# Squares and sub-norm factors moved to ScalarE, adaptive weights requested together, other tiles for the last expert

## The chip, the cores and the metric

The kernel runs on one core of a Trainium2 chip. A core has five engines that each work through their own list of instructions in order: TensorE (PE, matrix products; PEld in the profile is its weight load), VectorE (DVE), ScalarE (ACT), GpSimd (POOL) and SyncE (SP, which here issues nearly all DMA transfers). The metric is the device time of one execution in microseconds; less is better.

## The reference, cut to what matters

Two transformer blocks on 1024 tokens of width 1024, in fp32. The first has adaptive norms, a convolved two-way mLSTM with a Fourier branch, and 16 experts that each choose 128 tokens. The second has an even layer (differential attention A, forgetting attention B) and an odd layer (sliding window C, banded D). What the change touches:

```python
mx = (silu(c) @ w_ada + b_ada)[:, None, :]          # mc the same from c_ctx
sh1, sc1, ga1, sh2, sc2, ga2 = split(mx, 6)
pc = modulate(rmsnorm(ctx, g_norm1), csh1, csc1) @ w_in
px = modulate(rmsnorm(x, g_norm1), sh1, sc1) @ w_in
...
y = einsum('becf,efd->becd', hid, w_down) * vals    # experts: gather, SwiGLU, scatter-add
return zeros_like(h).at[bidx, idx].add(y)
...
aq, ak = rms_norm(aq, a_qn_g), rms_norm(ak, a_kn_g)  # per head of 64; the same for B, C, D
w = p[:, :, 0] - lam * p[:, :, 1]                    # A: difference of two softmaxes
o = rms_norm(einsum("bhqk,bkhe->bqhe", w, v), a_subln_g) * (1.0 - lam_init)
a_out = o * silu(ag)
```

## The kernel before, in words

A matrix product in fp32 is made of three products (`mm3`, L198 to L200): both operands are split into a high and a low part, the high part by a copy on ACT (L205) and the low part by a subtraction on DVE (L210). So each weight tile costs ACT about as long as DVE, and TensorE works three times. The framework puts each engine's instructions in one fixed order. An instruction waits for what it reads, and for its buffer: a tile name has a small number of buffers, and the next use of one waits for the last reader.

**The start** (`start`). Tokens (`x`, four tiles of 128x1024 first) are scaled by their norm, transposed by TensorE, and kept as `xr`. The adaptive vectors come from eight blocks of `w_ada` (128x8x256, 1 MB each, `wt`): five are multiplied on TensorE (L395, 16 narrow instructions a block), blocks 0, 2 and 5 on DVE (L387, L389, 16 each). From their sum come shift `sh` and scale `A` (L421 to L423). `modulated` (L344 to L347) then makes `y`, its high part `hh` and its low part `hl`; the first weight chunk's product (`pV`) starts when the first `hh` is there. `wt` has four buffers, so blocks 4 to 7 are loaded as blocks 0 to 3 are used up.

**The experts.** Expert e's gate, up and down products go through PSUM tiles `pge`, `pue`, `pde` (one buffer each). DVE scales a down product into `ye` (one buffer), and POOL scatter-adds it to memory in two halves (`xacc`, L1150). The last expert goes through `last_down` (L1153 on): both column halves c0 and c1 are computed apart, each one scaled by DVE (L1164) and scattered at once. Block 2 reads the sum back (`nx`).

**Block 2** is a planned stream of slots: attention items and, between them, the weight products of the next unit. Units A run from about 1470 to 1820 us, B to 2030, an output product, then key/value products, C, and D to the end. A unit's query/key chunk is evicted by ACT as `zq` (L1497); POOL squares it into `hsq` (L1504, one buffer); DVE sums the squares per head (L1505). The same buffer holds `osq` (L2001), ACT's squares of an attention result in A. In A the gates (`vg`) are multiplied by the sub-norm weights on POOL (L1724), and after four row blocks by the sub-norm's reciprocal roots `ory` (L1708, POOL, 128x512). `mixed` transposes the gated result and ACT evicts it as `so` (L1576). POOL also clears `ql` (L1542).

Of the kernel before, what the change touches and what calls it, by code (L numbers as in the profile page):

```python
# [47 lines left out]
def host_arrays(i):  # L48
    f = np.float32
# [42 lines left out]
    for q in range(4):  # L92
# [23 lines left out]
        "gln_o": g["odd_ln_g_2"][0],  # L116
        "subln": g["a_subln_g_2"][0],
        "gcols": np.concatenate([col(g["g_final"]), col(g["even_ln_g_2"][0])], axis=1),
# [39 lines left out]
class Kern:  # L158
# [154 lines left out]
    def start(self, P, hp, cp, xr):  # L313
# [10 lines left out]
        def load_x(t):  # L324
            xs[t] = P.tile([128, D], F32, name="x", bufs=6)
            src = a["x"][t * 128:(t + 1) * 128, :] if t < NT else a["ctx"][(t - NT) * 128:(t - NT + 1) * 128, :]
            nc.sync.dma_start(out=xs[t], in_=src)

        def load_w(b):
            wts[b] = P.tile([128, 8, 256], F32, name="wt", bufs=4)  # L330
            nc.sync.dma_start(out=wts[b], in_=a["w_ada"][b])

        self.hl, self.cl = Slabs([[None] * 2 for k in range(8)], 512), Slabs([[None] for k in range(8)], CTX)

        def modulated(k, g, x):

            c, hi, lo, pool, n = (0, self.hh, self.hl, hp, 512) if g < 2 else (1, self.ch, self.cl, cp, CTX)
            y = P.tile([128, 512], F32, name="y", bufs=3)[:, :n]
            h = hi[:, k, g % 2 * n:(g % 2 + 1) * n]
            if g:  # L340
                nc.scalar.activation(y, x, AF.Identity, bias=sh[:, k, c:c + 1], scale=A[:, k, c:c + 1])
                (nc.gpsimd.tensor_copy(h, y) if k % 3 == 2 else nc.scalar.activation(h, y, AF.Copy))
            else:
                nc.vector.tensor_scalar(y, x, A[:, k, c:c + 1], sh[:, k, c:c + 1], op0=OP.mult, op1=OP.add)  # L344
                nc.scalar.activation(h, y, AF.Copy)
            l = lo.tiles[k][g % 2] = pool.tile([128, n], F32R, name=f"hl{k}{g}" if c == 0 else f"cl{k}")
            (nc.gpsimd if k % 3 == 2 and g == 0 else nc.vector).tensor_tensor(l, y, h.bitcast(F32), op=OP.subtract)  # L347

# [27 lines left out]
        def ada(b):  # L376
            w = wts.pop(b)
            pc = self.ps.tile([128, 2, 2], F32, name="pc", tag="nu", bufs=3)
            if b in ON_DVE or b in ON_POOL:
                eng = nc.vector if b in ON_DVE else nc.gpsimd  # L380
                both = P.tile([128, 512], F32, name="ac", tag="y", bufs=3)
                for c in range(2):
                    ac = both[:, c * 256:(c + 1) * 256]
                    for k in range(8):
                        f = cs[:, k, c:c + 1]
                        if k == 0:
                            eng.tensor_scalar(ac, w[:, k], f, None, op0=OP.mult)  # L387
                        else:
                            eng.scalar_tensor_tensor(ac, w[:, k], f, ac, op0=OP.mult, op1=OP.add)  # L389
                    for i in range(2):  # L390
                        nc.tensor.matmul(pc[:, i, c:c + 1], ac[:, i * 128:(i + 1) * 128], one, start=True, stop=True)
            else:
                pa = self.ps.tile([128, 512], F32, name="pa", tag="mm", bufs=3)
                for k in range(8):
                    nc.tensor.matmul(pa[:2, :256], cs[:, k], w[:, k], start=k == 0, stop=k == 7)  # L395
                row = P.tile([2, 256], F32, name="arow", bufs=2)
                nc.vector.tensor_copy(row, pa[:2, :256])
                for i in range(2):
                    nc.tensor.transpose(pc[:, i], row[:, i * 128:(i + 1) * 128], self.ident[:2, :2])
            nc.vector.tensor_copy(ad[:, 2 * b:2 * b + 2], pc)  # L400

        for t in range(4):
            load_x(t)
        for b in range(4):
            load_w(b)
        tokens(0)
        for b in range(8):
            ada(b)
            if b + 4 < 8:
                load_w(b + 4)  # L410
            if b in (2, 3):
                self.stream[0].dma(b - 2)
        for t in range(4, 10):
            load_x(t)
        for j in range(2):
            self.stream[0].split(j, "pool")
        sh = P.tile([128, 8, 2], F32, name="sh")
# [642 lines left out]
    def experts(self, s):  # L1060
# [92 lines left out]
        def last_down(e):  # L1153
            pd = self.ps.tile([128, D], F32, name="pde", tag="pde", bufs=1)
            y = xp.tile([128, D], F32, name="ye", bufs=1)
            xh, xl = hs.pop(e)
# [198 lines left out]
    def even_consts(self, s):  # L1355
# [6 lines left out]
        pl = self.ps.tile([128, 512], F32, name="pl", tag="tr")  # L1362
        self.sub = ep.tile([128, 128], F32, name="sub")
        ones = ep.tile([64, 128], F32, name="lamo")
# [9 lines left out]

        def later():
            nc.gpsimd.dma_start(out=self.sub, in_=a["subln"].unsqueeze(0).to_broadcast([128, 128]))
            nc.gpsimd.tensor_scalar(self.sub, self.sub, 1.0 - lam_init, None, op0=OP.mult)
            nc.gpsimd.dma_start(out=self.cm, in_=a["cmask"])

        self.event(1, later)  # L1380
        self.ga = ep.tile([128, 4], F32, name="ga")
# [84 lines left out]
class Unit:  # L1466
# [33 lines left out]
    def squares(self, t, n):  # L1500
        K, nc, i = self.K, self.K.nc, t % 4
        sq = K.ap_.tile([128, 256], F32, name="hsq", tag="hsq", bufs=1)
        z = self.zq[t // 4][:, i, :n * 64]
        nc.gpsimd.tensor_tensor(sq[:, :n * 64], z, z, op=OP.mult)  # L1504
        nc.vector.tensor_reduce(self.ss[t // 4][:, i, :n], sq[:, :n * 64].rearrange("p (n d) -> p n d", d=64), op=OP.add, axis=mybir.AxisListType.X)  # L1505
# [57 lines left out]
    def mixed(self, g):  # L1563
# [10 lines left out]
        for i in range(2):  # L1574
            so = K.ap_.tile([128, 256], F32, name="so", tag="oxt", bufs=2)
            nc.scalar.activation(so, pt[:, i * 256:(i + 1) * 256], AF.Copy, scale=0.5)  # L1576
            nc.sync.dma_start(out=self.mx[self.u][:, g * 512 + i * 256:g * 512 + (i + 1) * 256], in_=so)
# [109 lines left out]
class UnitA(Unit):  # L1687
# [11 lines left out]
    def done(self, b):  # L1699
# [6 lines left out]
        r = K.rsqrt(K.up, ss, [128, 4], "or")  # L1706
        gt = self.gt[:, g * 4:g * 4 + 4]
        nc.gpsimd.tensor_tensor(gt, gt, r.unsqueeze(2).to_broadcast([128, 4, 128]), op=OP.mult)  # L1708
        K.event(K.slot_no + 2, lambda: self.mixed(g))

    def heads_in(self, ps, t, n):
        super().heads_in(ps, t, n)
        if self.h == 0:
# [311 lines left out]
```

## Time and profile before

| | us |
|---|---|
| three runs | 2799.67, 2801.87 (median), 2805.9 |
| the profiled execution, its own time | 2794.87 |
| its span in the trace | 2792.8 |
| outside the span | 2.07 |
| TensorE busy | 2649.0 (95%) |
| VectorE busy | 2006.8 (72%) |
| ScalarE busy | 1346.2 (48%) |
| GpSimd busy | 303.8 (11%) |

The granted clock of TensorE over the span is 0.984 of full speed. The busy share is an average over stages. The profile's line numbers are those of the kernel before; the changed code has the same statements a few lines further down.

### The profile page before, as it was taken

How to read it: one execution, taken by the hardware profiler on the slowest of the kernel's cores; microseconds unless marked ns; L12 is line 12 of the kernel's file. 1: busy time of each engine (PE TensorE's matmuls, PEld its weight loads, DVE VectorE, ACT ScalarE, POOL GpSimd, SP SyncE). 2: the span in 40 equal slices, each digit the busy share in tenths (PEclk: the TensorE clock that was granted, in tenths of full speed). 3: DMA queues.
4: the chain of work that ended last, by engine and by line, in shares of the span. 5: the costliest groups of instructions: out<-in, count | busy, mean ns of one | idle time of the engine just before them, and what ended most of it. 6: DMA issues, size and time to landing. Idle time of an engine off the chain costs nothing.

```text
span 2792.8 us, 48578 instructions
## 1 busy us (share of the span) xinstructions
PE 2649.0 (95%) x18222; PEld 2412.0 (86%) x18222; DVE 2006.8 (72%) x4981; ACT 1346.2 (48%) x2589; POOL 303.8 (11%) x413
## 2 busy tenths in 40 slices
PE   6999999999975999999979999999999999999999
PEld 3998897788974888888868999999989999999999
DVE  6676775558468999999968777766674777766652
ACT  4422332223233888877756545444453356544440
POOL 1000000000011111111122212111110000100000
PEclk9999999999987999999989999999999999999999
DMA  6222856655648999999942111211134322221143
GB/s 242 70 87 88 250 176 213 217 195 181 213 156 321 362 395 394 395 395 386 361 124 77 46 47 54 62 58 54 54 98 147 107 80 68 75 63 59 52 115 100
DMA packets 229708, 463.41 MB, mean 166 GB/s; under 512 B 19217, under 2 KB 121777, under 8 KB 228450
## 3 DMA queue, kind: packets, MB, share of 16 engines
q1 hardware_dynamic: 213218, 427.68, 43.9%
q0 software_dynamic: 7296, 17.96, 2.7%
q10 hardware_dynamic: 8960, 14.69, 2.3%
q8 instruction: 143, 2.34, 0.4%
q14 instruction: 91, 0.75, 0.1%
HBM read 387.80 MB, written 55.67 MB: 159 GB/s over the span
## 4 chain that ended last, share of the span: by engine, by line
PE 76%; DVE 10%; DMA 4%; issue 4%; ACT 4%; POOL 1%; SPq 1%; ACTq 0%; DVEq 0%; POOLq 0%
PE pz L198 7%; PE pz L200 7%; PE pz L199 7%; PE po L1954 5%; PE pT L199 3%; PE pT L198 3%; PE pT L200 3%; PE ptp L1940 2%; PE pge L198 2%; PE pge L200 2%; PE pge L199 2%; PE pue L199 2%; PE pue L200 2%; PE pue L198 2%; PE pde L199 2%
## 5 line engine op out<-in xcount | busy, mean ns | idle before, releaser
L198 PE MATMUL pz<-lwh,lh 128*128 128x256 f32 (+1 forms) x2368 | 678.6, 287 | 6.6 <-ACT lh L205 5.0
L200 PE MATMUL pz<-lwh,ll 128*128 128x256 f32 (+1 forms) x2368 | 668.2, 282 | 3.1 <-DVE ll L210 2.0
L199 PE MATMUL pz<-lwl,lh 128*128 128x256 f32 (+1 forms) x2368 | 670.7, 283 | 0.0
L198 PEld LDWEIGHTS pz<-lwh,lh 128*128 128x128 f32 x2368 | 448.2, 189 | 11.2 <-ACT lh L205 6.4
L200 PEld LDWEIGHTS pz<-lwh,ll 128*128 128x128 f32 x2368 | 448.0, 189 | 5.1 <-DVE ll L210 3.5
L199 PEld LDWEIGHTS pz<-lwl,lh 128*128 128x128 f32 x2368 | 449.1, 190 | 1.9
L210 DVE TENSOR_TENSOR ewl<-ewr,ewh 128x1024 fp32r<-128x1024 f32 x372 | 435.3, 1219 | 11.0 <-ACT ewh L205 4.7
L205 ACT ACTIVATE ewh<-ewr 128x1024 fp32r<-128x1024 f32 x378 | 390.6, 1061 | 74.7 <-PE pue L200 23.4
L1923 ACT ACTIVATE S<-S,mx 128x128 f32<-128x128 f32 (+2 forms) x192 | 125.8, 655 | 176.1 <-DVE mx L1898 144.7
L205 ACT ACTIVATE lwh<-lwr 128x1024 fp32r<-128x1024 f32 x130 | 135.8, 1054 | 99.8 <-PE pT L199 47.6
L210 DVE TENSOR_TENSOR lwl<-lwr,lwh 128x1024 fp32r<-128x1024 f32 x128 | 155.7, 1222 | 33.8 <-ACT lwh L205 33.1
L1954 PE MATMUL po<-vg,PT 128*128 128x64 f32 (+1 forms) x1344 | 173.6, 271 | 1.7 <-DVE PT L1945 1.2
L1887 DVE CUSTOM_DVE_ANT_0 S<-psc,bias 128x512 f32<-128x512 f32 (+3 forms) x336 | 161.4, 495 | 14.3 <-PE psc L1885 13.3
L1954 PEld LDWEIGHTS po<-vg,PT 128*128 128x128 f32 x1344 | 165.4, 192 | 5.2 <-ACT PT L1947 2.4
L198 PE MATMUL pT<-hh,lwh 128*128 128x512 f32 x384 | 155.8, 406 | 0.0
L199 PE MATMUL pT<-hl,lwh 128*128 128x512 f32 x384 | 153.3, 399 | 0.0
L200 PE MATMUL pT<-hh,lwl 128*128 128x512 f32 x384 | 152.6, 397 | 0.0
L1504 POOL TENSOR_TENSOR hsq<-zq 128x256 f32<-128x256 f32 (+1 forms) x136 | 84.7, 623 | 560.4 <-ACT zq L1497 267.2
L1884 PE MATMUL psc<-kY,qh 128*128 128x512 f32 (+3 forms) x352 | 128.4, 369 | 12.5 <-DVE mx L1887 9.9
L1940 PE MATMUL ptp<-pack,S 128*128 128x128 f32 x792 | 132.3, 276 | 7.4 <-ACT so L1576 4.6
L1150 POOL DMA_INDIRECT xacc<-ye,idx x32 | 70.5, 2203 | 437.4 <-DVE ye L1145 426.0
L1961 DVE SCALAR_TENSOR_TENSOR vg<-po,l,vg 128x64 f32<-128x64 f32 x192 | 54.0, 281 | 83.4 <-PE po L1954 81.8
(577 smaller groups left out, 6165.6 us busy)
## 6 DMA issues: line engine op xcount, KB each, us to landing
ewr<-in_w_gate_e SPq DMA_DIRECT2D x63, 1024.0 KB
ewr<-in_w_up_e SPq DMA_DIRECT2D x63, 1024.0 KB
ewr<-in_w_down_e SPq DMA_DIRECT2D x63, 1024.0 KB
lwr<-in_w_in SPq DMA_DIRECT2D x36, 512.0 KB
awt<-in_w_ada SPq DMA_DIRECT2D x32, 512.0 KB
lwr<-in_even_w_in SPq DMA_DIRECT2D x32, 512.0 KB
lwr<-in_odd_w_in SPq DMA_DIRECT2D x26, 512.0 KB
wt<-in_w_ada SPq DMA_DIRECT2D x8, 1024.0 KB
```

The costliest lines, as they stand in the source:

```text
L198: nc.tensor.matmul(out, ah, bh, start=start, stop=False)
L199: nc.tensor.matmul(out, ah, bl, start=False, stop=False)
L200: nc.tensor.matmul(out, al, bh, start=False, stop=stop)
L205: nc.scalar.activation(hi, raw, AF.Copy)
L210: (nc.vector if lo_eng == "dve" else nc.gpsimd).tensor_tensor(lo, raw, hi.bitcast(F32), op=OP.subtract)
L1150: nc.gpsimd.indirect_dma_start(out=self.xacc[c][:, :], out_offset=bass.IndirectOffsetOnAxis(ap=idx[:, e:e + 1], axis=0), in_=y[:, c * 512: ...
L1504: nc.gpsimd.tensor_tensor(sq[:, :n * 64], z, z, op=OP.mult)
L1884: nc.tensor.matmul(ps[:, :n], qh, k[:, ks], start=True, stop=False)
L1887: nc.vector.tensor_tensor_reduce(S[:, lo:hi], ps[:, lo - c0:hi - c0], bias, scale, -3e38, OP.add, OP.max, accum_out=mx[:, n_mx:n_mx + 1])
L1923: nc.scalar.activation(S[:, :nk], S[:, :nk], AF.Exp, bias=m, accum_out=l[:, 0:1])
L1940: nc.tensor.transpose(pt[:, i * 128:(i + 1) * 128], S[:, c0 + i * 128:c0 + (i + 1) * 128], K.ident)
L1954: nc.tensor.matmul(po[:, :dv], self.PT[i // 4][:, (i % 4) * 128:(i % 4 + 1) * 128], v(self.k0 // 128 + i), start=i == 0, stop=i == m - 1)
```

## The change

In `start` all eight blocks of `w_ada` are requested at once, ahead of the first chunk's weights and the other tokens. Blocks 0 to 4 get five `wt` buffers; 5 and 6 arrive in four pieces and 7 in eight, in tiles that later hold `hl` and `cl`. `x` has four buffers in place of six. POOL does nothing there any more: the two weight subtractions (L210) and the `hl` subtractions go to DVE, the casts to ACT, and the odd `y` of the second token group stay on ACT while the even ones go to DVE.

In `last_down` the product uses `pge` and the scaled rows use a buffer of the gathered rows `xe`.

In block 2 `squares` uses ACT. The sub-norm weights, now one column, are the scale of the `so` eviction; the multiplication of the gates by them is gone. The factor `ory` is applied by four ACT copies of 128x128. The mask `cm` is loaded by SP.

```diff
         def load_w(b):
-            wts[b] = P.tile([128, 8, 256], F32, name="wt", bufs=4)
-            nc.sync.dma_start(out=wts[b], in_=a["w_ada"][b])
+            if b < 5:
+                w = P.tile([128, 8, 256], F32, name="wt", bufs=5)
+                nc.sync.dma_start(out=w, in_=a["w_ada"][b])
+                wts[b] = [w[:, k] for k in range(8)]
+                return
+            wts[b] = []
+            for i in range(4 if b < 7 else 8):
+                n = 2 if b < 7 else 1
+                w = hp.tile([128, n, 256], F32, name=f"wt{b}{i}", tag=f"hl{(b - 5) * 4 + i}1") if b < 7 else cp.tile([128, n, 256], F32, name=f"wt{b}{i}", tag=f"cl{i}")
+                nc.sync.dma_start(out=w, in_=a["w_ada"][b][:, n * i:n * i + n])
+                wts[b] += [w[:, k] for k in range(n)]
...
-            if g:
+            if g == 2 or g and k % 2:
                 nc.scalar.activation(y, x, AF.Identity, bias=sh[:, k, c:c + 1], scale=A[:, k, c:c + 1])
-                (nc.gpsimd.tensor_copy(h, y) if k % 3 == 2 else nc.scalar.activation(h, y, AF.Copy))
             else:
                 nc.vector.tensor_scalar(y, x, A[:, k, c:c + 1], sh[:, k, c:c + 1], op0=OP.mult, op1=OP.add)
-                nc.scalar.activation(h, y, AF.Copy)
+            nc.scalar.activation(h, y, AF.Copy)
...
-            (nc.gpsimd if k % 3 == 2 and g == 0 else nc.vector).tensor_tensor(l, y, h.bitcast(F32), op=OP.subtract)
+            nc.vector.tensor_tensor(l, y, h.bitcast(F32), op=OP.subtract)
...
-        for b in range(4):
+        for b in range(8):
             load_w(b)
+        for j in range(2):
+            self.stream[0].dma(j)
         tokens(0)
         for b in range(8):
             ada(b)
-            if b + 4 < 8:
-                load_w(b + 4)
-            if b in (2, 3):
-                self.stream[0].dma(b - 2)
         for t in range(4, 10):
             load_x(t)
         for j in range(2):
-            self.stream[0].split(j, "pool")
+            self.stream[0].split(j)
...
         def last_down(e):
-            pd = self.ps.tile([128, D], F32, name="pde", tag="pde", bufs=1)
-            y = xp.tile([128, D], F32, name="ye", bufs=1)
+            pd = self.ps.tile([128, D], F32, name="pde", tag="pge", bufs=1)
+            y = xp.tile([128, D], F32, name="ye", tag="xe")
...
         z = self.zq[t // 4][:, i, :n * 64]
-        nc.gpsimd.tensor_tensor(sq[:, :n * 64], z, z, op=OP.mult)
+        nc.scalar.activation(sq[:, :n * 64], z, AF.Square)
...
-            nc.scalar.activation(so, pt[:, i * 256:(i + 1) * 256], AF.Copy, scale=0.5)
+            nc.scalar.activation(so, pt[:, i * 256:(i + 1) * 256], AF.Copy, scale=K.sub if self.kind == "a" else 0.5)
...
-        gt = self.gt[:, g * 4:g * 4 + 4]
-        nc.gpsimd.tensor_tensor(gt, gt, r.unsqueeze(2).to_broadcast([128, 4, 128]), op=OP.mult)
+        for i in range(4):
+            gt = self.gt[:, g * 4 + i]
+            nc.scalar.activation(gt, gt, AF.Copy, scale=r[:, i:i + 1])
...
-    def gate_in(self, t):
-        super().gate_in(t)
-        K = self.K
-        K.nc.gpsimd.tensor_tensor(self.gt[:, t], self.gt[:, t], K.sub, op=OP.mult)
```

Three places where the order of instructions differs. The first is VectorE at the end of the adaptive vectors (`arow` and `ad` are a block's row and its transposed columns, `lwl` the low part of the first chunk's weights). Before:

```order
L389 SCALAR_TENSOR_TENSOR ac<-wt,cs,ac 128x256 x9
L397 COPY arow<-pa 2x256
L400 COPY ad<-pc 128x4 x2
L397 COPY arow<-pa 2x256
L400 COPY ad<-pc 128x4
L422 TENSOR_TENSOR A<-ad,pack_100 128x16
L423 SCALAR_TENSOR_TENSOR A<-A,pack_100 128x16
L344 TENSOR_SCALAR y<-xr_89,A,sh 128x512
```

Now:

```order
L406 COPY arow<-pa 2x256
L409 COPY ad<-pc 128x4 x2
L406 COPY arow<-pa 2x256
L210 TENSOR_TENSOR lwl<-lwr,lwh 128x8x128
L409 COPY ad<-pc 128x4
L429 TENSOR_TENSOR A<-ad,pack_100 128x16
L430 SCALAR_TENSOR_TENSOR A<-A,pack_100 128x16
L210 TENSOR_TENSOR lwl<-lwr,lwh 128x8x128
L353 TENSOR_SCALAR y<-xr_89,A,sh 128x512
```

The two weight subtractions, which POOL had, now stand between the last block's row and the first `y`.

The second place is ScalarE in a unit A, around the end of a row group (`S` are the exponentials of a row block, `PT` the transposed weights on their way out of PSUM). Before:

```order
L1984 ACTIVATE S,l<-S,mx 128x896 x2
L1497 ACTIVATE zq<-pz 128x256 x2
L1576 ACTIVATE so<-ptm 128x256 x2
L1497 ACTIVATE zq<-pz 128x256
L2001 ACTIVATE osq,oss<-po,l 128x128
L1947 ACTIVATE PT<-ptp 128x256
L1984 ACTIVATE S,l<-S,mx 128x1024 x2
```

Now:

```order
L1983 ACTIVATE S,l<-S,mx 128x896 x2
L1712 ACTIVATE vg<-vg,ory 128x128 x4
L1500 ACTIVATE zq<-pz 128x256
L1507 ACTIVATE hsq<-zq 128x256
L1500 ACTIVATE zq<-pz 128x256
L1507 ACTIVATE hsq<-zq 128x256
L1579 ACTIVATE so<-ptm,sub 128x256 x2
L1500 ACTIVATE zq<-pz 128x256
L1507 ACTIVATE hsq<-zq 128x256
L2000 ACTIVATE osq,oss<-po,l 128x128
L1946 ACTIVATE PT<-ptp 128x256
L1983 ACTIVATE S,l<-S,mx 128x1024 x2
```

A square follows each `zq`, and the four factor copies stand ahead of the `so` evictions.

The third is VectorE at the same `osq` (`mx` is a row maximum, `ISA` the instruction that adds the bias and takes it). Before:

```order
L1520 TENSOR_TENSOR hry<-hry,rt 128x16
L1523 TENSOR_TENSOR zq<-zq,hry 128x256 x4
L1505 TENSOR_REDUCE hss<-hsq 128x4
L2003 SCALAR_TENSOR_TENSOR vg<-po,l,vg 128x128
L1945 COPY PT<-ptp 128x512
L1887 ISA S,mx<-psc,bias 128x512
```

Now:

```order
L1523 TENSOR_TENSOR hry<-hry,rt 128x16
L1526 TENSOR_TENSOR zq<-zq,hry 128x256 x4
L1508 TENSOR_REDUCE hss<-hsq 128x4
L1944 COPY PT<-ptp 128x512
L2002 SCALAR_TENSOR_TENSOR vg<-po,l,vg 128x128
L1886 ISA S,mx<-psc,bias 128x512
```

The copy of `PT`, which does not depend on `osq`, now stands ahead of the multiplication that does.

## Rows read from the trace of the kernel before

**Rows 1.** The page: engine busy times, and VectorE's weight subtractions in the first stages.

```profile
PE 2649.0 (95%) x18222; PEld 2412.0 (86%) x18222; DVE 2006.8 (72%) x4981; ACT 1346.2 (48%) x2589; POOL 303.8 (11%) x413
...
L210 DVE TENSOR_TENSOR lwl<-lwr,lwh 128x1024 fp32r<-128x1024 f32 x128 | 155.7, 1222 | 33.8 <-ACT lwh L205 33.1
```

**Rows 2.** Windows of the core: busy by engine (instructions), TensorE clock, DMA share, GB/s.

```profile
20.00:30.00 10.00, 10.00 (x57) 5.25 (x56) 7.18 (x21) 3.94 (x8) 0.00 (x0) 1.00 0.42 129
...
40.00:50.00 10.00, 7.48 (x31) 3.11 (x30) 4.18 (x10) 3.36 (x5) 3.26 (x2) 0.83 1.01 409
...
1400.00:1470.00 70.00, 56.12 (x252) 45.57 (x251) 43.49 (x60) 36.95 (x55) 16.62 (x12) 0.83 0.43 123
1610.00:1680.00 70.00, 66.65 (x535) 64.36 (x533) 53.98 (x187) 34.90 (x87) 14.29 (x22) 1.00 0.16 45
1890.00:1960.00 70.00, 70.00 (x590) 69.02 (x589) 44.59 (x168) 31.40 (x67) 12.97 (x23) 1.00 0.20 62
```

**Rows 3.** Timeline of TensorE, start: start, duration, line, names, [idle before <-released by].

```profile
33.97 2.75 PE L395 MATMUL pa<-wt,cs 128*2 128x256 f32 x12
...
42.71 0.58 PE L391 MATMUL pc<-one,ac 128*128 128x1 f32 x4 [2.52 <-DVE ac L389]
...
44.96 5.30 PE L395 MATMUL pa<-wt,cs 128*2 128x256 f32 x16
...
53.03 0.39 PE L198 MATMUL pV<-lwh,hh 128*128 128x272 f32 x1 [1.99 <-ACT hh L345]
...
55.62 0.39 PE L200 MATMUL pV<-lwh,hl 128*128 128x272 f32 x1 [0.47 <-POOL hl L347]
```

**Rows 4.** Timeline of VectorE, start.

```profile
37.62 5.86 DVE L389 SCALAR_TENSOR_TENSOR ac<-wt,cs,ac 128x256 f32<-128x256 f32 x9
...
51.77 1.46 DVE L344 TENSOR_SCALAR y<-xr,A,sh 128x512 f32<-128x512 f32 x3
```

**Rows 5.** Timeline of TensorE, last expert.

```profile
1419.84 0.47 PE L198 MATMUL pde<-ewh,xth 128*128 128x512 f32 x1 [1.86 <-DVE ye L1145]
...
1432.02 0.76 PE L198 MATMUL pde<-ewh,xth 128*128 128x512 f32 x1 [4.87 <-DVE ye L1164]
```

**Rows 6.** Timeline of VectorE, last expert.

```profile
1431.12 0.75 DVE L1164 SCALAR_TENSOR_TENSOR ye<-pde,val,ga 128x512 f32<-128x512 f32 x1 [6.90 <-DMA xacc<-ye,idx]
...
1440.54 0.75 DVE L1164 SCALAR_TENSOR_TENSOR ye<-pde,val,ga 128x512 f32<-128x512 f32 x1 [5.87 <-PE pde L200]
```

**Rows 7.** Timeline of GpSimd, last expert.

```profile
1441.58 1.70 POOL L1150 DMA_INDIRECT xacc<-ye,idx  x1 [2.15 <-DVE nlam L1372]
```

**Rows 8.** Waits of TensorE, units A: total us, times, longest.

```profile
PE psc L1884 <- DVE mx L1887: 9.9, 9, 1.7
...
PE ptp L1940 <- ACT so L1576: 3.3, 3, 1.2
```

**Rows 9.** Timeline of TensorE, around one osq of a unit A.

```profile
1629.53 0.50 PE L1884 MATMUL psc<-kY,qh 128*128 128x512 f32 x1 [1.73 <-DVE mx L1887]
```

**Rows 10.** Timeline of ScalarE, the same place in a unit A.

```profile
1627.42 0.37 ACT L2001 ACTIVATE osq<-po,l 128x128 f32<-128x128 f32 x1 [2.61 <-DVE hss L1505]
```

**Rows 11.** Timeline of VectorE, two places in a unit A.

```profile
1605.15 0.42 DVE L1505 TENSOR_REDUCE hss<-hsq 128x4 f32<-128x256 f32 x1 [0.92 <-POOL hsq L1504]
...
1624.75 0.18 DVE L193 SCALAR_TENSOR_TENSOR hry<-hrt,hry 128x16 f32<-128x16 f32 x1
1624.96 0.58 DVE L1520 TENSOR_TENSOR hry<-hry,rt 128x16 f32<-128x16 f32 x1
```

**Rows 12.** Instructions of ScalarE's squares in the output product.

```profile
L1645 ACT ACTIVATE hsq<-oxt x12: 407/418/419, 2085.6 to 2171.2; 128x256 f32<-128x256 f32 x12
```

**Rows 13.** Instructions of the squares' line: ns min/median/max.

```profile
L1504 POOL TENSOR_TENSOR hsq<-zq x136: 398/612/1628, 1468.0 to 2636.2; 128x256 f32<-128x256 f32 x104, 128x128 f32<-128x128 f32 x32
```

**Rows 14.** Timeline of GpSimd, end of a row group, unit A.

```profile
1577.92 1.04 POOL L1708 TENSOR_TENSOR vg<-vg,ory 128x512 f32<-128x512 f32 x1 [5.36 <-DVE ory L193]
```

**Rows 15.** Table loads of ScalarE at the gates' line.

```profile
L1510 ACT ACT_TABLE_LOAD  x1: 1283/1283/1283, 1504.1 to 1504.1; - x1
```

More of the change, by code (lines that the diff above doesn't have):

```diff
@@ L33, in _pack @@
     PACK_W[which] += n
-for _n, _w in (("ident", 128), ("bbf", 8), ("qkg", 8), ("lam", 4), ("sinks", 8), ("cc", 16)):
+for _n, _w in (("ident", 128), ("bbf", 8), ("qkg", 8), ("lam", 4), ("sinks", 8), ("cc", 16), ("subln", 1)):
     _pack(_n, _w, 0)
@@ L80, in host_arrays @@
     put("ident", np.eye(128, dtype=f))
+    put("subln", g["a_subln_g_2"][0][:, None])
     s, j = np.meshgrid(np.arange(128), np.arange(128), indexing="ij")
@@ L116, in host_arrays @@
         "gln_o": g["odd_ln_g_2"][0],
-        "subln": g["a_subln_g_2"][0],
         "gcols": np.concatenate([col(g["g_final"]), col(g["even_ln_g_2"][0])], axis=1),
@@ L324, in load_x @@
         def load_x(t):
-            xs[t] = P.tile([128, D], F32, name="x", bufs=6)
+            xs[t] = P.tile([128, D], F32, name="x", bufs=4)
             src = a["x"][t * 128:(t + 1) * 128, :] if t < NT else a["ctx"][(t - NT) * 128:(t - NT + 1) * 128, :]
@@ L386, in ada @@
                         if k == 0:
-                            eng.tensor_scalar(ac, w[:, k], f, None, op0=OP.mult)
+                            eng.tensor_scalar(ac, w[k], f, None, op0=OP.mult)
                         else:
-                            eng.scalar_tensor_tensor(ac, w[:, k], f, ac, op0=OP.mult, op1=OP.add)
+                            eng.scalar_tensor_tensor(ac, w[k], f, ac, op0=OP.mult, op1=OP.add)
                     for i in range(2):
@@ L394, in ada @@
                 for k in range(8):
-                    nc.tensor.matmul(pa[:2, :256], cs[:, k], w[:, k], start=k == 0, stop=k == 7)
+                    nc.tensor.matmul(pa[:2, :256], cs[:, k], w[k], start=k == 0, stop=k == 7)
                 row = P.tile([2, 256], F32, name="arow", bufs=2)
@@ L1362, in even_consts @@
         pl = self.ps.tile([128, 512], F32, name="pl", tag="tr")
-        self.sub = ep.tile([128, 128], F32, name="sub")
+        self.sub = ep.tile([128, 1], F32, name="sub")
         ones = ep.tile([64, 128], F32, name="lamo")
@@ L1373, in even_consts @@
         self.cm = ep.tile([128, 128], F32, name="cm")
[L1375 to L1380, printed above, removed]
+        self.event(1, lambda: nc.sync.dma_start(out=self.cm, in_=a["cmask"]))
+        nc.vector.tensor_scalar(self.sub, self.col("subln"), 0.5 * (1.0 - lam_init), None, op0=OP.mult)
         self.ga = ep.tile([128, 4], F32, name="ga")
```

## The prediction, made before the changed kernel ran

> **What bounds the kernel now.** I began with the page: TensorE is busy for 95% of the span, every other engine for 72% or less [rows 1]. So an edit pays only where TensorE stands idle or runs at the lower of its two clocks (1.2 against 2.4 GHz). The windows say where that is [rows 2]: at the start, 7.48 of 10 us busy at a granted clock of 0.83 between 40 and 50; where the experts end, 56.12 of 70 us, again at 0.83; a little in units A, 66.65 of 70. Units B are full, 70.00 of 70. Then I read in the timelines and waits of those three places what ended each wait.
>
> **The start.** Between 40 and 50 us TensorE first waits 2.52 us for block 5's products on VectorE, and then multiplies block 7 for 5.30 us, where twelve such instructions took 2.75 before it, 0.229 each, so that sixteen are worth 3.67 [rows 3]. The engine had just been idle when the clock fell. The link is not the limit: it is full between 40 and 50, yet 0.42 busy between 20 and 30, where TensorE works without a pause [rows 2]. With all blocks requested at once their data come early enough for block 5 (nine of its VectorE steps, which took 5.86 us [rows 4], can run sooner and without GpSimd beside them) and blocks 6 and 7 follow each other. I take off the wait and the slow stretch: 2.52 + 1.63 = 4.15 us.
>
> Against it VectorE takes over GpSimd's two weight subtractions, 1.22 us each [rows 1], and the order puts both between block 7's row and the first `y`, which stood at 51.77 [rows 4]. Behind it waits TensorE's first `pV` (53.03, 1.99 us idle [rows 3]). Of the 2.44 us about 0.5 fill a pause in which VectorE waits for block 7's columns; 1.94 are added. GpSimd's `hl` subtractions go: two waits like that of 0.47 at 55.62 [rows 3], -0.94. The `ctx` tokens now load only when `x`'s four buffers come free, and their scaling comes late: no row shows it, it costs between nothing and 1.46 us (three 128x512 passes of VectorE [rows 4]); I take 0.65, near the middle, since transposes of other tokens cover part. On SP the eight blocks now stand ahead of the first weights, which lie ready long before `pV` either way. Sum: -4.15 + 1.94 - 0.94 + 0.65 = -2.5 us. Bounds: +1.6 if the slow clock merely moves to the first product (+1.63) and `ctx` costs its 1.46; -6 if the subtractions hide entirely.
>
> **The last expert.** Its first half waits 1.86 us, because `pde` is still read by VectorE's scaling of the expert before; the second half waits 4.87 us [rows 5], because VectorE could not write `ye` (it waited 6.90 us for the scatter that still reads it) and so did not release the first half's sums [rows 6]. With `pge` and an `xe` buffer neither applies: -6.73 us. The first half took 7.31 us (1419.84 to 1432.02 less 4.87), the second 8.52 (to 1440.54); without the pause in front of it the second should be no slower than the first, -1.2. Together -7.9. What is late next is the scatter: the second half's started at 1441.58 [rows 7]. A scatter into the same half of `xacc` follows the former expert's, which had landed by 1431.12 [rows 6]; two more of some 1.7 to 2.3 us put the second one's start near 1433.4, 8.2 us earlier. Both ways give 8, and I take -8 (between -5, if the landing of one half holds the other, and -10, if the whole tail runs at full clock). `sub` and `cm` leave GpSimd's list ahead of the last scatter; `cm` goes to SP in block 2, where it is one small transfer.
>
> **Units A.** TensorE waits there 9.9 us for row maxima in nine waits and 3.3 us for `so` [rows 8].
> The longest wait, 1.73 us [rows 9], I followed back: ACT's `osq` had waited 2.61 us [rows 10] for VectorE's sum, since both squares share `hsq`; VectorE was held up by a 128x16 multiplication that took 0.58 us beside GpSimd's square, where the one before it took 0.18 [rows 11]; and the copy of `PT` stood behind the product with `osq`. Now GpSimd is silent (0.40 less) and the copy stands ahead (at least `osq`'s 0.37 and its read-out, about 0.6): 1.0 us in each of four units, -4.0.
> Three waits of about 0.7 began with VectorE waiting 0.92 us for the square [rows 11]; ACT's takes 0.42 [rows 12] where GpSimd's median is 0.61 and its worst 1.63 [rows 13], and no gate multiplication stands in front: -2.1.
> The `so` wait grows: in front of it ACT now makes four factor copies of 128x128. With a scale from a tile such an instruction took 0.37 (`osq` [rows 10]), so 1.48 against GpSimd's 1.04 [rows 14], +0.44, less a little contention: +0.3 in four units, +1.2. Sum -5 us; bounds -11 (most of the 13.2) and +2 (nothing gained, `so` grows by 0.44 four times).
> The Trainium skill (ScalarE: Activation LUTs, What ACT_TABLE_LOAD costs) says that each operand taken as a 128x1 pointer adds about 93 ns to an instruction, which would lengthen the `so` evictions too, now that their scale is a column; by it two of them in each of eight groups add 1.5 us, and the sum would be -3.5. No row here shows an eviction with both forms, so it stays out of my sum.
>
> **Units B, C, D and the key/value products.** 104 of the 136 squares lie here. ScalarE has room (31.40 of 70 us in units B [rows 2]), and TensorE's window is full: nothing to gain. I take 0, since 0.42 us behind a `zq` delays no row maximum by itself; from -3 (contention gone) to +6 (one square in seven on TensorE's path).
>
> **Sum.** -2.5 - 8 - 5 = -15.5 us. The profiled execution took 2794.87 (2.07 outside its span), which gives 2779.4. It lies 7.0 us, 0.25%, below the median of the runs; against 2801.87 I predict 2786.4, and give 2786.
>
> **Rivals.**
> *ScalarE becomes the wait (slower).* A square on ACT may write `hsq` only after VectorE's sum of the one before it, and that sum can stand behind weight subtractions of 1.22 us [rows 1]. GpSimd could wait there without harm; behind a waiting ACT stand the exponentials and `PT` evictions that TensorE needs. At 0.42 us [rows 12] every second one of the 104 outside units A adds 22 us: 2801.9 - 15.5 + 22 = 2808. From 0.15 us a square on it eats the whole gain. For it: one buffer, and B's TensorE has no slack to hide it. Against: ACT is under half busy in units B, and products of several microseconds lie between two `zq`. Chance 0.11.
> *The squares reload ScalarE's tables (slower).* If squares and exponentials needed different tables, each square would bring two loads of 1.283 us [rows 15]: 136 x 2.57 = 349 us, 3135. Against: the only load at the gates' line is at 1504.1, and `osq`, also a square, comes hundreds of microseconds later between exponentials [rows 10]. Chance 0.01. The Trainium skill (ScalarE: Activation LUTs, Table sets: the hidden batching unit) warns of such reloads when functions of different sets alternate; the trace shows that these do not.
> *The waits change their owner (no change).* The start gives nothing, since both subtractions land on the path; units A give nothing, since `so` takes over; the last expert gives only 5, as the scatters end late. 2797. For it: the start's price is certain and its gain is not. Chance 0.14.
> *The last expert's halves wait on.* Both halves lie in one PSUM tile, so the second may still wait for VectorE's read of the first; VectorE has 1.22 us subtractions ahead of that. Then -7.5 in all, 2794. Against: 4.87 us came from `ye`, which is another buffer now. Chance 0.06.
> *The transfers were the limit at the start.* The link's free 58% between 20 and 30 us [rows 2] are 5.8 us; had they bounded it, all would move up by that: 2801.9 - 15.5 - 5.8 = 2781. Against: TensorE's pauses there are for VectorE. Chance 0.08.
>
> **How the numbers follow.** The forecast has 0.60. About 0.2%, 5.6 us, is what a measurement of this kernel tells from no change. Faster: 0.60 + 0.06 + 0.08 = 0.74; within: 0.14; slower: 0.12. The bounds of the four terms add up to -30 and +4.6, which is 2772 and 2806; the slower rivals lie beyond the upper end with 0.12, and the run-to-run spread adds a little below. For 8 in 10 I give 2770 to 2806.
>
> **What would show it.** Right: no wait of 2.5 us before 45 us; `pV` near 50.8; the last expert's `pge` products without a wait over 1 us and the last scatter near 1433 plus the start's shift; no 1.73 us waits in units A, `so` waits of 1.1 to 1.5. Wrong: ACT's squares with waits for VectorE's sums, and TensorE waiting for `PT` of ACT in units B or D; half clock in the first `pV` products; GpSimd's last scatter within 3 us of where it was.

## The result, and the profile after

The changed kernel takes 2770.81 us (median; 2764.52 to 2772.05) against 2801.87: the ratio is 0.9887, 95% interval 0.9873 to 0.9902, or 31 us less. The forecast was 2786 us with a range of 2770 to 2806, so the time lies at the very end of the range. The direction was right, and the gain is twice the forecast. Its profiled execution took 2772.05, with a span of 2770.3.

The two profiled executions differ by only 22.8 us. To see where, I compared the start of the same TensorE instruction in both traces; the change of that difference over a stage is what the stage gained (minus is faster):

| stage (us in the trace before) | forecast | measured |
|---|---|---|
| start, to 100 | -2.5 | -3.0 |
| 100 to 1400, the same instructions in the same order | 0 | +8.9 |
| last expert and block 2's start, 1400 to 1480 | -8 | -9.0 |
| units A, 1480 to 1830 | -5 | -17.5 |
| the rest | 0 | -2.0 |

The +8.9 is no price of the change. The experiments below show the same stretch 0.0 to 11.1 us later than in the profile before, 6 on average: that profiled execution was a quick one (2794.87, where the median is 2801.87). Against a usual execution the change gains its 31 us. A stage's figure from one trace has a spread of its own: units A of e12, whose instructions are those of the changed kernel, read -15.4, and those of e1, e2, e7 and e8, which are those of the kernel before, -0.3 to +1.3.

The page of the changed kernel, its engine line, which answers to [rows 1]:

```profile
PE 2648.1 (96%) x18222; PEld 2415.1 (87%) x18222; DVE 1990.5 (72%) x4990; ACT 1396.8 (50%) x2757; POOL 178.6 (6%) x226
```

TensorE does the same work in a shorter span; ScalarE has 51 us more, GpSimd 125 less. The windows of the changed kernel, as in [rows 2]:

```profile
40.00:50.00 10.00, 5.90 (x29) 2.65 (x28) 5.39 (x13) 1.06 (x3) 0.00 (x0) 0.96 0.18 53
50.00:60.00 10.00, 10.00 (x59) 9.88 (x59) 9.54 (x19) 8.35 (x15) 0.00 (x0) 0.70 0.29 79
1400.00:1470.00 70.00, 58.09 (x295) 48.08 (x294) 51.59 (x69) 45.41 (x69) 10.26 (x8) 0.90 0.41 128
1610.00:1680.00 70.00, 69.26 (x558) 67.14 (x557) 53.48 (x197) 42.28 (x109) 2.08 (x4) 1.00 0.19 54
1890.00:1960.00 70.00, 69.76 (x586) 68.64 (x585) 46.77 (x183) 35.99 (x82) 8.52 (x19) 1.00 0.23 69
```

Units A went from 66.65 busy of 70 to 69.26, nearly as full as units B (69.76). At the start the slow stretch moved: between 50 and 60 us the granted clock is now 0.70, part of it at 1.2 GHz, after a pause of TensorE. The timeline of VectorE and TensorE there, for [rows 3, 4]:

```profile
45.62 1.20 DVE L210 TENSOR_TENSOR lwl<-lwr,lwh 128x1024 fp32r<-128x1024 f32 x1
...
47.23 1.22 DVE L210 TENSOR_TENSOR lwl<-lwr,lwh 128x1024 fp32r<-128x1024 f32 x1
48.37 1.45 DVE L353 TENSOR_SCALAR y<-xr,A,sh 128x512 f32<-128x512 f32 x3
```

```profile
42.49 2.75 PE L404 MATMUL pa<-wt,cs 128*2 128x256 f32 x12
45.75 0.28 PE L408 MATMUL pc<-pack,arow 2*128 2x2 f32 x2 [0.51 <-DVE arow L406]
49.63 0.60 PE L198 MATMUL pV<-lwh,hh 128*128 128x272 f32 x1 [3.60 <-ACT hh L354]
```

Block 7 runs at full speed and without a wait, and `pV` starts 3.4 us earlier than at 53.03. But both subtractions stand ahead of `y`, and the pause of 3.60 us is followed by the slow clock.

The last expert, TensorE and then GpSimd, for [rows 5, 7]:

```profile
1430.92 0.47 PE L198 MATMUL pde<-ewh,xth 128*128 128x512 f32 x1 [1.37 <-DVE ye L1171]
...
1443.90 2.52 PE L1229 MATMUL ptn<-pack,nx 128*128 128x128 f32 x7 [6.95 <-DMA nx<-xacc]
```

```profile
1432.11 2.37 POOL L1157 DMA_INDIRECT xacc<-ye,idx  x1 [1.69 <-DVE ewl L210]
1437.71 1.56 POOL L1157 DMA_INDIRECT xacc<-ye,idx  x1 [3.24 <-DVE nlam L1379]
```

The waits of 1.86 and 4.87 us are gone but for 1.37; what is late next is the read of the summed rows `nx`, 6.95 us.

The waits of TensorE in units A (total, times, longest), for [rows 8]:

```profile
PE ptp L1939 <- ACT so L1579: 1.3, 3, 0.7
PE pth L1532 <- DVE zq L1526: 0.9, 1, 0.9
PE ptp L1939 <- DVE PT L1944: 0.8, 4, 0.2
PE psc L1883 <- DVE mx L1886: 0.5, 2, 0.3
PE pth L1532 <- ACT so L1579: 0.5, 1, 0.5
```

Row maxima fell from 9.9 us to 0.5, and `so` fell too, though it was to grow. VectorE's own waits for the squares, in the kernel before and in the changed one:

```profile
DVE hss L1505 <- POOL hsq L1504: 20.1, 18, 2.4
```

```profile
DVE hss L1508 <- ACT hsq L1507: 10.0, 10, 2.4
```

The place of [rows 9 to 11] in the changed kernel, VectorE and then ScalarE:

```profile
1613.31 0.18 DVE L1523 TENSOR_TENSOR hry<-hry,rt 128x16 f32<-128x16 f32 x1
1613.52 1.43 DVE L1526 TENSOR_TENSOR zq<-zq,hry 128x256 f32<-128x256 f32 x4
1614.87 0.41 DVE L1508 TENSOR_REDUCE hss<-hsq 128x4 f32<-128x256 f32 x1
1615.20 0.68 DVE L1944 COPY PT<-ptp 128x512 f32<-128x512 f32 x1
```

```profile
1613.72 0.42 ACT L1507 ACTIVATE hsq<-zq 128x256 f32<-128x256 f32 x1
1615.38 0.37 ACT L2000 ACTIVATE osq<-po,l 128x128 f32<-128x128 f32 x1 [1.24 <-DVE hss L1508]
```

The 128x16 multiplication takes 0.18 in place of 0.58, the copy of `PT` is ahead, and TensorE does not wait here at all. ScalarE's new instructions by line (ns min/median/max):

```profile
L1507 ACT ACTIVATE hsq<-zq x136: 297/416/511, 1465.9 to 2614.2; 128x256 f32<-128x256 f32 x104, 128x128 f32<-128x128 f32 x32
...
L1712 ACT ACTIVATE vg<-vg,ory x32: 385/387/403, 1536.8 to 1781.9; 128x128 f32<-128x128 f32 x32
...
L1579 ACT ACTIVATE so<-ptm x40: 360/374/387, 1815.4 to 2630.2; 128x256 f32<-128x256 f32 x40
...
L1579 ACT ACTIVATE so<-ptm,sub x16: 455/466/476, 1539.9 to 1785.7; 128x256 f32<-128x256 f32 x16
```

Each costs what the prediction took (0.42 and 0.37). The `so` eviction with a column as its scale takes 0.466 against 0.374 with a constant: 92 ns, which agrees with the 93 ns that the Trainium skill (ScalarE: Activation LUTs, What ACT_TABLE_LOAD costs) gives for a pointer operand.

### The profile page after: what moved, and what is told of

Its sections match the earlier page's. It is cut to its first block, busy times and chain, and to the rows that moved or that the text cites. A ratio compares the mean times of both kernels' runs of the same rounds, so it can differ in the third digit from the quotient of the medians.

```text
span 2770.3 us, 48439 instructions
## 1 busy us (share of the span) xinstructions
PE 2648.1 (96%) x18222; PEld 2415.1 (87%) x18222; DVE 1990.5 (72%) x4990; ACT 1396.8 (50%) x2757; POOL 178.6 (6%) x226
## 4 chain that ended last, share of the span: by engine, by line
PE 66%; DVE 8%; DMA 4%; ACT 3%; issue 2%; POOL 0%; SPq 0%; ACTq 0%; DVEq 0%; POOLq 0%
PE pz L198 8%; PE pz L200 8%; PE pz L199 8%; PE po L1953 5%; PE ptp L1939 3%; PE pue L199 2%; PE pue L200 2%; PE pge L198 2%; PE pue L198 2%; PE pge L199 2%; PE pge L200 2%; PE pde L199 2%; PE pde L200 2%; PE pde L198 2%; PE psc L1883 2%
## 5 line engine op out<-in xcount | busy, mean ns | idle before, releaser
L210 DVE TENSOR_TENSOR ewl<-ewr,ewh 128x1024 fp32r<-128x1024 f32 x372 | 435.4, 1220 | 12.2 <-ACT ewh L205 5.9
L210 DVE TENSOR_TENSOR lwl<-lwr,lwh 128x1024 fp32r<-128x1024 f32 x130 | 158.4, 1222 | 43.7 <-ACT lwh L205 43.0
L198 PE MATMUL pV<-lwh,hh 128*128 128x256 f32 (+1 forms) x384 | 111.1, 290 | 3.6 <-ACT hh L354 3.6
L1884 PE MATMUL psc<-kY,ql 128*128 128x512 f32 (+3 forms) x352 | 111.0, 332 | 0.4 <-DMA ql<-ql 0.4
```

The source lines that it names most:

```text
L198: nc.tensor.matmul(out, ah, bh, start=start, stop=False)
L210: (nc.vector if lo_eng == "dve" else nc.gpsimd).tensor_tensor(lo, raw, hi.bitcast(F32), op=OP.subtract)
L1884: nc.tensor.matmul(ps[:, :n], ql, k[:, ks], start=False, stop=True)
```

## The experiments

### Each part alone

**e1_start** (only the start), **e2_last** (only `last_down`), **e3_squares** and **e4_subnorm**, each put into the kernel before. The edits of the last two:

```diff
# e3_squares
-        nc.gpsimd.tensor_tensor(sq[:, :n * 64], z, z, op=OP.mult)
+        nc.scalar.activation(sq[:, :n * 64], z, AF.Square)
# e4_subnorm
...
-            nc.scalar.activation(so, pt[:, i * 256:(i + 1) * 256], AF.Copy, scale=0.5)
+            nc.scalar.activation(so, pt[:, i * 256:(i + 1) * 256], AF.Copy, scale=K.sub if self.kind == "a" else 0.5)
...
-        gt = self.gt[:, g * 4:g * 4 + 4]
-        nc.gpsimd.tensor_tensor(gt, gt, r.unsqueeze(2).to_broadcast([128, 4, 128]), op=OP.mult)
+        for i in range(4):
+            gt = self.gt[:, g * 4 + i]
+            nc.scalar.activation(gt, gt, AF.Copy, scale=r[:, i:i + 1])
...
-    def gate_in(self, t):
-        super().gate_in(t)
-        K = self.K
-        K.nc.gpsimd.tensor_tensor(self.gt[:, t], self.gt[:, t], K.sub, op=OP.mult)
```

The lines left out of e4 load the sub-norm weights as one column and the mask `cm` by SP. The 13.8 us of units A in these expectations count from 1500 us; from 1480 it is 17.5.

> The kernel before with the change of the start alone. In the changed kernel the first chunk's products are 3.0 us earlier by 100 us of the trace, and 5.9 us later by 900 us, although the order of instructions between is the same. Theory 1 (the later loss is a matter of where the slow-clock stretches fall, and not of the start): here the shift at 100 us is -3.0 again, and the shifts near 480, 515 and 825 us differ from those of the changed kernel by several us in either direction; time -3, from -8 to +5. Theory 2 (the start's other DMA order makes the middle later): the same +5.9 at 900 us and a time 3 to 6 us longer than before.

> The kernel before with last_down's other tiles alone. Theory 1 (the two waits of 1.86 and 4.87 us and the scatter behind them set the start of block 2): 8 to 9 us off the local stretch from 1400 to 1480 us, time -8 (-4 to -12). Theory 2 (block 2 waits for the scatters' landing however early the products end): -4 to -5 us, with a wait of TensorE for nx of 5 us or more.

> The kernel before with the squares on ScalarE alone; the gate multiplications stay on GpSimd. Theory 1 (it was the squares on GpSimd, slow and beside VectorE, that held row maxima up): units A from 1480 to 1820 us lose 9 to 10 of the 13.8 us that the changed kernel saves there, time -10. Theory 2 (the sub-norm multiplications on GpSimd were the cause, in front of the squares in GpSimd's list and beside VectorE): 4 us or less. Units B and the odd layer within 3 us by both.

> The kernel before with the sub-norm weights at the eviction and the factors on ScalarE alone; the squares stay on GpSimd. Theory 1 (squares are the cause): 3 to 5 us off units A. Theory 2 (the gate multiplications were the cause): 9 us or more. The two parts together with e3 should give 13.8; if both alone give more than that in sum, the same waits are removed twice, if less, each needs the other (a silent GpSimd).

| | ratio (95%) | to 100 | 100 to 1400 | to 1480 | units A | rest |
|---|---|---|---|---|---|---|
| changed | 0.9887 (0.9873, 0.9902) | -3.0 | +8.9 | -9.0 | -17.5 | -2.0 |
| e1_start | 0.9980 (0.9968, 0.9993) | -3.6 | +3.4 | +0.4 | +0.4 | -1.3 |
| e2_last | 0.9980 (0.9968, 0.9992) | +1.5 | +7.2 | -7.5 | +1.3 | +3.5 |
| e3_squares | 0.9933 (0.9913, 0.9952) | +1.7 | +7.5 | -2.8 | -15.6 | -2.2 |
| e4_subnorm | 0.9974 (0.9961, 0.9987) | +2.4 | +4.5 | +0.3 | -5.2 | -1.1 |

All four gain, and their sum, 1.33%, is near the whole, 1.13%. The squares are half of it. In e1 the middle is +3.4 and in e3, whose start is the old one, +7.5: the start does not make the middle late. The old starts (e2, e3, e4, e6, e7, e8) lie 1.1 to 2.4 us behind the one profiled before, so the start is worth some 5 us; e1's ratio gives 5.6, between 2 and 9. In units A the two parts alone sum to 20.8, more than the 17.5 together, which suggests that some waits are removed by either. Without the factor copies on ScalarE `so` nearly ceases to delay TensorE; the waits of e3_squares:

```profile
PE psc L1884 <- DVE mx L1887: 2.4, 6, 0.9
PE psc L1884 <- DMA kY<-klo: 1.0, 2, 0.6
PE ptp L1940 <- DVE PT L1945: 0.8, 4, 0.2
PE pth L1529 <- DVE zq L1523: 0.8, 1, 0.8
PE pz L200 <- DVE ll L1225: 0.7, 1, 0.7
PE ptp L1940 <- ACT so L1576: 0.5, 1, 0.5
```

### Contention or queueing in units A

**e5_gpsimd_beside**: GpSimd repeats the squares beside the changed kernel's.

```diff
         nc.scalar.activation(sq[:, :n * 64], z, AF.Square)
+        m = min(n * 64, 224)
+        scr = K.ap_.tile([128, 224], mybir.dt.bfloat16, name="scr", tag="scr", bufs=1)
+        nc.gpsimd.tensor_tensor(scr[:, :m], z[:, :m], z[:, :m], op=OP.mult)
```

> The changed kernel, and beside each square on ScalarE GpSimd squares the same zq again (224 of the 256 columns, into a scratch tile that nobody reads). VectorE, ScalarE and TensorE have the same instructions in the same order as in the changed kernel. Theory C (contention: VectorE's two-input instructions were slow beside GpSimd, and that held the row maxima up): units A from 1480 to 1820 us get 4 us or more of the gain back, with small VectorE instructions of 0.5 us and more beside GpSimd. Theory Q (queueing: only that others waited for GpSimd's result, in its place in the list): units A stay within 1.5 us of the changed kernel.

Units A gain 9.7 us over the kernel before, where the changed kernel gains 17.5: GpSimd's squares, for which the other engines wait 0.3 us in all there, cost 7.9. So theory C holds, and theory Q alone does not. The other 9.6 us would then be theory Q's share, the wait for GpSimd's results in their place in the lists; no run shows that share by itself. The ratio is 0.993 (0.991, 0.995). The place of [rows 11] here, GpSimd and then VectorE:

```profile
1621.45 0.82 POOL L1510 TENSOR_TENSOR scr<-zq 128x224 bf16<-128x224 f32 x1 [2.66 <-DVE hry L1526]
```

```profile
1621.42 1.80 DVE L1529 TENSOR_TENSOR zq<-zq,hry 128x256 f32<-128x256 f32 x4
```

Four multiplications take 1.80 us instead of 1.43. Of the 7.9 us, 4.5 are lost before 1555, in the first unit. TensorE's wait for `zq` there is 2.20 us, where the changed kernel has 0.9:

```profile
1490.36 0.62 PE L1535 MATMUL pth<-pack,zq 128*128 128x128 f32 x2 [2.20 <-DVE zq L1529]
```

In the 10 us ahead of it four instructions of VectorE take some 1.3 us more than in the changed kernel, each beside a square of GpSimd. One of them has a single tensor input and takes 0.50 us instead of 0.17:

```profile
1486.35 0.50 DVE L1524 TENSOR_SCALAR hss<-hss 128x16 f32<-128x16 f32 x1
```

Behind the wait the granted clock of the window 1490 to 1500 is 0.83, as in the kernel before, where the changed kernel has 1.00, and TensorE waits 1.87 us for a DMA transfer of `kY`. Whether these two follow from the contention is not shown: e12, with nothing added on GpSimd, has 0.83 between 1510 and 1520.

Nor is it GpSimd's time as such that costs. In units A it is about as busy in e3_squares, with the gate multiplications, as in e5 (43.45 and 44.73 us, the last busy time before the clock), and e3 gains 15.6 us all the same:

```profile
1470.00:1830.00 360.00, 353.21 (x2830) 341.97 (x2830) 283.52 (x1024) 216.73 (x533) 43.45 (x73) 1.00 0.20 59
```

```profile
1470.00:1830.00 360.00, 348.59 (x2789) 337.06 (x2788) 279.28 (x1015) 220.28 (x549) 44.73 (x74) 1.00 0.21 59
```

The squares stand beside the short instructions that lead up to `zq`, for which TensorE waits; that this place makes the difference is argued and was not tried.

**e6_osq_own**: e4_subnorm with a buffer of its own for `osq`.

```diff
-        sq = K.ap_.tile([128, 256], F32, name="osq", tag="hsq", bufs=1)[:, :128]
+        sq = K.ap_.tile([128, 128], mybir.dt.bfloat16, name="osq", tag="osq", bufs=1)
```

> The kernel before with the sub-norm part, and osq in a buffer of its own, so that ScalarE's square of an attention result no longer waits for VectorE's sum of GpSimd's square; the squares stay on GpSimd. Theory Q (the shared buffer was the chain): the four waits of 1.0 us for row maxima that e4_subnorm still has, of 1.02 to 1.08 each, go, 3 to 4 us less than e4_subnorm in units A. Theory C (contention on VectorE): they stay above 0.6 us each and units A change by less than 1.5 us.

By theory Q the 1.0 us waits should go; they stay at 1.05 to 1.06, as theory C says. `osq` now starts 1.4 us after its product's first instruction, where it was 3.2 in e4, but VectorE is late all the same, with 0.62 us for the 128x16 multiplication beside GpSimd. What the shared buffer had cost at this place is the 0.7 us from 1.73 to 1.02, and e4 has that already, because the copy of `PT` stands ahead there; in e6 it stands behind again. Units A -3.7, against -5.2 in e4, within the spread of such figures; ratio 0.9986 (0.9972, 1.0). **e10_osq_own_after** has the same edit in the changed kernel.

> The changed kernel with osq in a buffer of its own. ScalarE's osq still waits 9.8 us there for VectorE's sums, but TensorE's remaining waits for row maxima in units A are below 0.4 us each. By the theory that only TensorE's waits count: units A gain 0 to 1.5 us, the time is the changed kernel's within 3 us. By the rival that ScalarE's head of line is the next bound: 3 us or more less in units A.

Units A -16.5, ratio 0.9907 (0.9885, 0.9930): nothing gained, as expected where only TensorE's waits count.

### The last expert

**e7_pge** and **e8_xe** have one of the two tiles each, in the kernel before:

```diff
# e7_pge
-            pd = self.ps.tile([128, D], F32, name="pde", tag="pde", bufs=1)
+            pd = self.ps.tile([128, D], F32, name="pde", tag="pge", bufs=1)
# e8_xe
-            y = xp.tile([128, D], F32, name="ye", bufs=1)
+            y = xp.tile([128, D], F32, name="ye", tag="xe")
```

> The kernel before with last_down's product in the pge tile, its scaled rows still in the single ye. By the theory that ye set the longer wait: only the first half's 1.86 us wait goes, the second half still waits for the scatter of the expert before, and its wait grows by what the first saved, 6 to 7 us; local stretch from 1400 to 1480 us within 2 us of the kernel before. By the rival that the PSUM tile set both: 5 us or more off.

> The kernel before with last_down's scaled rows in an xe buffer, its product still in pde. By the theory that ye set the longer wait: the second half's wait of 4.87 us goes or falls below 2, the first half's 1.86 stays, 5 to 6 us off the stretch from 1400 to 1480 us. By the rival that the scatters' landing decides: below 3 us off, with a longer wait for nx.

With `pge` alone the first half's wait goes and the second's grows:

```profile
1440.65 0.77 PE L198 MATMUL pde<-ewh,xth 128*128 128x512 f32 x1 [5.85 <-DVE ye L1164]
```

The stretch to 1480 gains 1.1 us (2805.32 in one run). With `xe` alone it gains 6.7 (2788.11 in one run), and the first half's 1.86 stays. So `ye` held the last expert up, and `pge` adds little.

The size is less certain than the cause, as GpSimd's scatter of the last expert but one has two lengths. It took 5.69 to 5.70 us in the kernel before and in e1 to e5, and 2.28 to 2.29 in the changed kernel and in e6 to e12. The kernel before, and e6, whose last expert is the same:

```profile
1419.97 5.69 POOL L1150 DMA_INDIRECT xacc<-ye,idx  x1 [42.65 <-DVE ye L1145]
```

```profile
1426.66 2.28 POOL L1150 DMA_INDIRECT xacc<-ye,idx  x1 [42.62 <-DVE ye L1145]
```

With the short scatter and the old tiles e6 reads -4.0 in the stretch to 1480, so that much of e8's 6.7 and of the changed kernel's 9.0 may be the scatter's. e7 and e8 both have the short one, and their difference of 5.6 us stands. With the long scatter the two new tiles read -7.5 (e2) and -4.4 (e5).

### The start, and an attempt at a better version

**e9_start_pool**: the changed kernel with the first chunk's subtractions on GpSimd.

```diff
-            self.stream[0].split(j)
+            self.stream[0].split(j, "pool")
```

> The changed kernel with the first chunk's two weight subtractions back on GpSimd (2.5 us each there). Theory 1 (the two subtractions of 1.22 us on VectorE between block 7's row and the first y cost their time): the first pV starts about 2 us earlier than the changed kernel's 49.6, and with the shorter pause the slow clock behind it may go, 2 to 4 us less by 100 us. Theory 2 (the pause is set by ScalarE's copy and TensorE's columns, or GpSimd's subtractions end later): no earlier start of pV. Time within 4 us of the changed kernel.

The start got 5.8 us worse (+2.8 to 100 us); ratio 0.9923 (0.9904, 0.9941). The pause ahead of `pV` is shorter, 1.99 us for 3.60, so the two subtractions do cost VectorE their place, as theory 1 says. But `pV` starts at 54.43, 4.8 us later: the outcome of theory 2, for a reason that neither names, contention. GpSimd, VectorE, TensorE:

```profile
33.43 4.85 POOL L210 TENSOR_TENSOR lwl<-lwr,lwh 128x1024 fp32r<-128x1024 f32 x2 [32.00 <-ACT lwh L205]
```

```profile
32.62 0.48 DVE L398 SCALAR_TENSOR_TENSOR ac<-wt,cs,ac 128x256 f32<-128x256 f32 x1
...
33.47 2.61 DVE L398 SCALAR_TENSOR_TENSOR ac<-wt,cs,ac 128x256 f32<-128x256 f32 x1
...
36.11 4.83 DVE L398 SCALAR_TENSOR_TENSOR ac<-wt,cs,ac 128x256 f32<-128x256 f32 x7
```

```profile
41.32 0.37 PE L408 MATMUL pc<-pack,arow 2*128 2x2 f32 x2 [3.77 <-DVE arow L406]
...
54.43 0.65 PE L198 MATMUL pV<-lwh,hh 128*128 128x272 f32 x3 [1.99 <-ACT hh L354]
```

A step of 0.48 us takes 2.61, about as long as the first of GpSimd's two subtractions beside it, and seven steps beside the second take 4.83, where the changed kernel has 2.85. The Trainium skill (SBUF — State Buffer, Who interferes with whom) says that a VectorE instruction with two SBUF inputs contends with a GpSimd one that reads SBUF, over a port pair that only one of them has at a time. The row of 2.61 us agrees.

**e11_early_split**: the first chunk's weights are requested ahead of blocks 6 and 7, and their subtractions are issued ahead of block 7's products, which puts both earlier in VectorE's order. **e12_early_two**: e11 with the last expert's halves in two PSUM tiles.

```diff
# e11_early_split
         for b in range(8):
+            if b == 6:
+                for j in range(2):
+                    self.stream[0].dma(j)
             load_w(b)
-        for j in range(2):
-            self.stream[0].dma(j)
         tokens(0)
         for b in range(8):
+            if b == 7:
+                for j in range(2):
+                    self.stream[0].split(j)
             ada(b)
...
-        for j in range(2):
-            self.stream[0].split(j)
# e12_early_two, besides
-            pd = self.ps.tile([128, D], F32, name="pde", tag="pge", bufs=1)
+            pds = [self.ps.tile([128, D], F32, name="pde", tag=tag, bufs=1) for tag in ("pge", "pue")]
...
+                pd = pds[c]
```

> The changed kernel with the first chunk's weights requested ahead of blocks 6 and 7, so that VectorE's two weight subtractions come before block 6's row, in a pause of VectorE. By the theory that they cost their place in the order: the first pV starts near 47.7 instead of 49.6, a pause of about 1.6 us instead of 3.6, and where the shorter pause keeps the full clock 2 us more; 2 to 5 us less by 100 us. By the rival that blocks 6 and 7 now come late: TensorE waits for them before 45 us and nothing is gained. Time from -6 to +1 of the changed kernel.

> e11_early_split, and the last expert's two column halves in PSUM tiles of their own (pge and pue), so that the second need not wait for VectorE's read of the first. By the theory that this read set the remaining 1.4 us wait there: the wait goes, the last scatter starts 1 to 1.5 us earlier against its own local time, and the stretch from 1400 to 1480 us is 1 us shorter than in e11_early_split. By the rival that the scatter before decides when the last can start: no change, TensorE's wait for nx longer by what was saved.

In e11 `pV` starts as expected:

```profile
47.86 0.59 PE L198 MATMUL pV<-lwh,hh 128*128 128x272 f32 x1 [1.92 <-ACT hh L354]
```

By 100 us of the trace e11 reads -5.8 and e12 -5.1, where the start of the changed kernel reads -3.0, and -4.9 and -4.2 in e5 and e10: up to 3 us more. The time does not follow: 0.9907 (0.9892, 0.9922). In e12 the second half's wait is gone and the last scatter's own wait is shorter, but TensorE waits 9.14 us for `nx` (9.22 in e11); the stretch to 1480 is 1.1 us shorter than e11's and longer than the changed kernel's; 0.9895 (0.9876, 0.9914). Neither beats the changed kernel by more than can be measured. A few microseconds of one stage are as much as the middle's spread.

## Why the prediction was right, and where its size was off

*The start*: the mechanism as predicted; 2.52 and 1.63 us went, both subtractions stand ahead of `y` (e11 puts their price at 1.8 us of `pV`'s start; the sum had 1.94). The slow clock moved to the first product, which the prediction had named as a sign of being wrong. The bound given for that, +1.6, counts the slow stretch twice: -2.5 + 1.63 + 0.81 (1.46 less the 0.65 of the sum) is about 0. The part was still worth some 5 us and not 2.5. GpSimd's contention with VectorE's products had no term of its own in the sum, and e9 shows what it can cost there.

*The last expert*: -9.0 for -8. The wait for `ye` was the term (e8 against e7), the read of `nx` is what is late next. That the size fits so well may be luck, as the trace of the changed kernel has the short scatter and that of the kernel before the long one; e2's ratio puts the part at 5.6 us, between 2 and 9.

*Units A* is the term that was mis-sized: -5 in the sum, -17.5 measured, beyond even the bound of -11. The time, 2770.81, lies below the 2772 to which all four lower bounds add up, and inside the range only by the little that was added for the spread of runs; that is luck. Three things in units A:
- "Now GpSimd is silent (0.40 less)" counted the contention only where I had followed one wait back. It slows VectorE at other places too; e5 puts it at 7.9 us with all that came behind it, more than half of them in the first unit, whose waits for `zq` I had left out of the sum (first of the two rows below, from the kernel before).
- "The `so` wait grows, +1.2." The price was right: 1.8 us with the factor copies against 0.5 in e3_squares, without them. But `so` stood at 4.4 us before (3.3 in [rows 8] and 1.1 in the second row below), and with the squares moved 0.5 of it is left in e3.
- The chain through the shared `hsq` was sized rightly: it held 0.7 of the 1.73 us (1.02 in e4, whose squares are still on GpSimd, and 1.05 in e6 by the other way); the sum had 0.6. The other 1.0 us went too, where I had counted 0.40: in the changed kernel VectorE comes to the 128x16 multiplication 0.20 us after TensorE begins that `po`, and not 0.72. That it comes earlier because it has waited less before is argued and not tried.

```profile
PE pth L1529 <- DVE zq L1523: 3.7, 2, 3.2
...
PE pth L1529 <- ACT so L1576: 1.1, 1, 1.1
```

*The rivals*: ScalarE did not become the wait. VectorE's sums still hold `osq` back for 9.8 us in all, and e10, which takes that away, gains nothing. The five table loads stayed five. "The last expert's halves wait on" came true for 1.37 us. B, C, D gave -2.0 for 0, which is no more than the spread: the same code reads -1.5 to +2.9 in e5 and e9 to e12.

*The base*: the sum was made against 2794.87 and carried to the median; that was right, since the profiled execution was 6 us quick in the untouched middle.

## What to carry to other kernels

In this kernel a small operation on GpSimd next to a busy VectorE was priced by what it did to VectorE's instructions beside it, and not by its own length: look for VectorE rows of one shape that take two or five times their median, over the whole stage, and ask for each whether TensorE waits behind it. As much GpSimd work in another place cost little (e3). A chain of waits names the last releaser only: freeing `osq` alone left the wait at 1.0 us, because VectorE was late by itself. And where stages are compared by one trace each, look first at a stage that was not changed: its difference is the measurement's.

## What was not expected of the hardware

With the same instructions in the same order, the stretch from 100 to 1400 us differed by up to 11 us between profiled executions. One pause goes with much of it. In six of the fourteen traces (the changed kernel, e3, e5, e7, e9, e10) TensorE stands idle for 1.7 to 2.0 us ahead of one product, and from it to the 40th instruction after it 12.9 to 13.8 us pass; in the other eight there is no pause and it is 8.8 to 9.5. The six are 7.5 to 11.1 us late in that stretch, the eight 0.0 to 7.2. In the changed kernel:

```profile
510.85 0.58 PE L199 MATMUL pd<-od1l,fh 128*128 128x256 f32 x1 [2.04 <-DVE od1l L210]
```

In the window 510 to 520 us the granted clock is 0.50 there, 0.67 in e10, and 1.00 in the kernel before, which has no such pause. Old and new starts are in both groups, so the change does not decide it. What makes VectorE late for that product was not followed.

The two lengths of GpSimd's scatter, 5.69 and 2.28 us, are the second thing: old and new tiles are in both groups, and why was not tried.
